# Windowed attention with its scores two blocks ahead, and the second key group projected one stage earlier

## The chip, the cores and the metric

The kernel runs on one core of a Trainium2 chip. The metric is the device time in microseconds from launch to end; the kernel before was run three times: 1077.41, 1073.83 and 1075.31, median 1075.31 us.

## The reference

One encoder layer over 1024 positions with 16 learned meta tokens ahead of them (T = 1040), model width 1024, everything in float32:

```python
u = _rms_norm(h, pre_w)
z = u @ w_in
rq, rk, rv, rg, aq, ak, av, ag, gr, ga = _split_in(z)
...
o_r = _bidirectional_retention(rq, rk, rv, lg_f, lg_b)      # 4 heads, forward and backward scan
...
y_r = (groupnorm(o_r) * ret_nw * silu(rg)) @ w_rb
...
aq = _rotary(aq) ; ak = _rotary(ak)                         # 8 query heads, 2 key groups, width 128
o_a = _windowed_sink_attention(aq, ak, av, sink)            # window +-128, meta keys, sink logit
y_a = (o_a * silu(ag)) @ w_ab
...
mix = sigmoid(gr) * y_r + sigmoid(ga) * y_a
return h + _rms_norm(mix @ w_o, post_w)
```

The attention takes, for each query, the keys within 128 positions and the 16 meta keys, adds a learned sink to the softmax's denominator and multiplies by the values of those keys.

## The kernel before

**Precision.** Each operand of TensorE is kept as a high part (type fp32r, made by a cast, on ScalarE as a rule) and a low part (made on VectorE by subtraction, `dve_lo`, line 90), and a product takes three matmuls: high by high, low by high, high by low (`mm3`, lines 74 to 76). What the text calls a step is one such group of three. A projection of 512 positions and 128 output columns is 8 steps (24 matmuls).

**Stages.** By the profile's times: set-up and first projection up to about 37 us; four retention heads up to 345 us; attention from 345 to 570 us; from there to 1066 us the gates and the three output products in a seven-product (Strassen-like) form; a short tail. The last retention head (head 3) runs from about 250 to 345 us.

**Attention.** There are 32 chunks: two key groups (g = 0, 1), and in each 16 blocks of 64 queries for the four heads of the group. A chunk has three stages.
- `stage1`: the scores. Two tiles `ps` on TensorE (six matmuls, in the two memory banks of the ring p2); VectorE adds the mask and takes the maximum (`raw`, `nm`, line 1366); ScalarE takes the exponential `p` (line 1369); VectorE inverts the sum (`den`, line 1372); GpSimd scales `p` (line 1379).
- `stage2`: the transposes `pt1`, `pt2` of p on TensorE (lines 1390, 1393; six instructions, in the two banks of the ring p1), then high parts on ScalarE (`pah`, `pbh`) and low parts on VectorE (`pal`, `pbl`). The banks come free for the next chunk when these four are done.
- `stage3`: p times values, `po` (nine matmuls, one bank), copied out by ScalarE (`oa`) and stored.

In TensorE's order the scores of chunk k+1 stand ahead of the transposes of chunk k. Then comes filler work, which does not depend on this chunk, and then `po` of chunk k-1. The filler is a list of generators (`works`), of which `fill(n)` issues n steps; `FILL` gives n for each chunk (7 or 8, in the last half 5). The list holds query projections (`paq`, from `gen_aq`), the projection of the second key group (`pak1`, from `gen_ak(1)`), and then products `pe` of the gates' weights (`gen_pre`, weights 6 to 13, each 24 matmuls), which the later stage loads back from DRAM.

Behind a step, the table `BEGUN` hangs other work: to fetch a weight (`fetch_aq`, `fetch_ak`), to split one half of it (`half_w`), to load, scale and subtract a piece of x and store it (`sum_fetch`, `sum_row`), to fetch a gate weight (`pre_fetch`: two transfers `we`), to sum its four parts (`pre_sums`, lines 785 to 787), and to split the sum (`pre_parts`: `weh` on ScalarE, line 794, then `wel` on VectorE). The two buffers for `we` are one pair: the next weight's transfers have to wait until this weight's sums and splits are done.

Queries are rotated (`rope_evac`: three multiplications on VectorE, lines 184 to 186, and an addition on GpSimd, line 187), stored to DRAM, and loaded again four heads at a time (`load_q`); `split_q` makes `aqh` on ScalarE (line 659) and `aql` on VectorE, two chunks before a pair of chunks needs them. Keys are rotated and split into `kT` (`keys`).

**What sets the order.** The kernel writes its own instruction order: each engine runs its queue in the order in which the program issues, and a pass that reorders within limits is bound by `issue_after` (`follow`), which puts an instruction's place behind that of others. SyncE (SP) issues nearly all transfers, in one queue.

Of the kernel before, what the change touches and what calls it, by code (L numbers as in the profile page):

```python
# [14 lines left out]
NM = 16  # L15
# [11 lines left out]
FILL = (7,) + (8,) * 6 + (7,) * 9 + (5,) * 15  # L27
# [12 lines left out]
def block_kernel(ctx: ExitStack, tc: tile.TileContext, xT, x, w_in, w_rb, w_ab, w_out, vecs, dec, sink,  # L40
# [68 lines left out]
    def halves_w(u):  # L109
        hi, lo = [], []  # L110

        def split(t, act):
            h, l = (wp.tile([P, 4, 256], R, tag=f"w{x}", bufs=4, name=f"w{x}{u}_{len(hi)}") for x in "hl")
            if act:
                nc.scalar.copy(h, t)
            else:
                pool_hi(h, t)
            dve_lo(l, t, h)
            hi.append(h)
            lo.append(l)  # L120

# [335 lines left out]
    def retention(h, fill):  # L457
# [137 lines left out]
        for c in range(NB, 0, -1):  # L595
# [67 lines left out]
    def fetch_aq(hp):  # L663
        raw = fetch_w(w_in, U_AQ + hp)
        split, wq[hp] = halves_w(U_AQ + hp)
        begun["q", hp] = lambda s: split(raw[s], True)

    def fetch_ak():
        raw = fetch_w(w_in, U_AK)
        split, w_ = halves_w(U_AK)  # L670
        wak.append(w_)
        begun["k", 1] = lambda s: split(raw[s], True)

    def half_w(which, i, s):
        begun[which, i](s)

    begun = {}

    def gen_aq(hp, i):
# [3 lines left out]
        for e_ in range(2):  # L683
            t = yield from proj(wq[hp], P * e_, a, b, f"paq{hp}_{i}{e_}")
            o = ra.tile([P, 512], F32, tag="q", bufs=6, name=f"aq{hp}_{i}{e_}")
            rope_evac(t, a, b, o, f"aq{hp}_{i}{e_}")
# [7 lines left out]
    rotated_k = {}  # L694

    def keys(g, i):
# [3 lines left out]
        kh, kl = (t[:, 2 * i:2 * i + 2, 0:P] for t in kT[g])  # L700
        o = rotated_k.pop((g, i))
        s = NM if i == 0 else 0
        x = o[:, s:s + 256].rearrange("p (t c) -> p t c", t=2)
        nc.scalar.copy(kh, x)
        dve_lo(kl, x, kh)
        if i == 0:
            mh, ml = (t[:, :, P:144] for t in kT[g])
            x = o[:, 0:NM].unsqueeze(1).to_broadcast([P, NB, NM])
# [18 lines left out]
    def sum_fetch(q):  # L727

        k, c = q // 2, slice(256 * (q % 2), 256 * (q % 2) + 256)
        for i in range(2):  # L730
            xsum[i] = t = ap.tile([P, 2, 256], F32, tag="xs", bufs=2, name=f"xs{i}{q}")
            nc.sync.dma_start(t, xT[4 * i + k, :, NM:T].rearrange("p (j t) -> p j t", j=2)[:, :, c])

    def sum_row(q):

        k, c = q // 2, slice(256 * (q % 2), 256 * (q % 2) + 256)
        x = {}
        for i, t in xsum.items():
            nc.scalar.activation(t, t, AF.Copy, scale=vec[:, 4 * i + k:4 * i + k + 1])
            for j in range(2):  # L740
                x[i, j] = t[:, j]
        for _, o, a, b in SUMS:
            nc.vector.tensor_tensor(x[o], x[a], x[b], ALU.subtract)
        for i, t in xsum.items():
# [44 lines left out]
    def pre_parts(u):  # L789
# [5 lines left out]
        dve_lo(l, t[:, :, 0:n], h)  # L795
        parts[u] = h, l

    def gen_pre(u):

        if u not in parts:  # L800
# [3 lines left out]
            pre_parts(u)  # L804
        h, l = parts.pop(u)
# [13 lines left out]
    def hooked(gens, at):  # L819

        n = 0
        for g in gens:
            for _ in g:
# [4 lines left out]
                yield  # L828
# [21 lines left out]
    for h in range(NH):  # L850
        fill, drain = filler([gen_qk(h + 1), pieces(pre, (4, 4, 8)[h])] if h < 3 else [gen_ak(0), gen_aq(0, 0), gen_aq(1, 0)])
# [476 lines left out]
    def attention():  # L1328
# [19 lines left out]
        def stage1(g, b):  # L1348
# [3 lines left out]
            den = ap.tile([P, 2], F32, tag="den", bufs=3, name=f"den{g}_{b}")  # L1352
            pt = []
            for e_ in range(2):
                hp, o0 = 2 * g + e_, 256 * (b % 2) + P * e_
                if (g, b // 2) not in aqs:
                    split_q(g, b // 2)
# [7 lines left out]
                p = ap.tile([P, 353], F32, tag="p", bufs=4, name=f"p{hp}_{b}")  # L1365
# [36 lines left out]
        def stage3(g, b):  # L1402
# [14 lines left out]
            if b % 2:  # L1417
# [6 lines left out]
        works = [gen_aq(1, 1), gen_aq(0, 1), gen_aq(2, 0), gen_aq(3, 0), gen_aq(2, 1), gen_aq(3, 1),  # L1424
                 gen_ak(1, (0, 1)), pieces(pre, 8), gen_ak(1, (2,)), pieces(pre, 8), gen_ak(1, (3,)), pre]
        fill = filler([hooked(works, BEGUN)])[0]
# [4 lines left out]
        with follow(last["pb"]):  # L1431
            next(av, None)
        edge_values(0, 0)
        edge_values(0, 1)

        with follow(*latest):
            fill(3)
        with follow(*latest):
            stage1(0, 0)
        for k, (g, b) in enumerate(chunks):  # L1440
            ends = k >= len(chunks) - 2
            if k + 1 < len(chunks):
                with follow(*latest, *marks("oa", "lo")):
                    stage1(*chunks[k + 1])
                if chunks[k + 1] == (0, 2 * NB - 1):
                    keys(1, 0)
            if k + 2 < len(chunks):
                edge_values(*chunks[k + 2])
            if chunks[k] == (1, 2 * NB - 2):

                with follow(*latest):
                    fill(FILL[k])
                yield
            if not k:
                with follow(*latest):
                    fill(FILL[k] - 3)
            with follow(*latest, *marks("exp", "sum")) if not ends else ExitStack():
                stage2(g, b)
            if k % 2 and k + 3 < len(chunks):
                g_, b_ = chunks[k + 3]  # L1460
                load_q(g_, b_ // 2)
            if k % 2 == 0 and k + 2 < len(chunks):
                g_, b_ = chunks[k + 2]
                with follow(*marks("exp", "sum", "lo", "hi")):
                    split_q(g_, b_ // 2)
            if k and not ends:
                with follow(*latest):
                    fill(FILL[k])
            with follow(*latest) if not ends else ExitStack():
                if k:  # L1470
                    stage3(*chunks[k - 1])
            if ends:
                yield
            if k in (12, 17, 21):
                x_to_out({12: 0, 17: 4, 21: 6}[k])
        stage3(*chunks[-1])


# [125 lines left out]
```

## Time and profile before

| | us |
|---|---|
| median of three runs | 1075.31 (1073.83 to 1077.41) |
| profiled execution | 1075.24 |
| its span, first to last instruction | 1073.5 |
| TensorE busy | 1049.6 (98%) |
| VectorE busy | 867.9 (81%) |
| ScalarE busy | 487.0 (45%) |
| GpSimd busy | 217.2 (20%) |
| mean granted TensorE clock | 0.995 |

The profiled execution is within 0.1 us of the median, and 1.74 us of it lie outside the span. The profile's engines are PE (TensorE), DVE (VectorE), ACT (ScalarE), POOL (GpSimd) and SP (the queue of transfers). In a table of windows each engine has its busy time and, in brackets, its instructions; then come the granted clock of PE, the share of the transfer engines that were busy, and GB/s. In a table of waits a row says which engine's instruction waited for whose result, the time in total, how often, and the longest.

### The profile page before, as it was taken

The page shows a single profiled execution, that of the slowest core. Times are in us where ns is not written, and L with a number is a line of the kernel's source. Part 1 is how long each engine was busy: PE and PEld are TensorE (multiplying, and loading weights), DVE is VectorE, ACT ScalarE, POOL GpSimd, SP SyncE. Part 2 cuts the span into 40 slices and gives each one's busy share as a digit, 9 for nine tenths or more (in the row PEclk, how much of TensorE's full clock was granted, in tenths as well). Part 3 has the DMA queues.
Part 4 walks back from the last instruction along what each step waited for, and adds up shares of the span by engine and source line. Part 5 has one row for each costly group of instructions (what it writes and reads, how often), then busy time and mean ns, then how long its engine had stood idle before and what let it go on. Part 6 is the DMA issues. An engine that isn't in the chain of part 4 may idle for free.

```text
span 1073.5 us, 17195 instructions
## 1 busy us (share of the span) xinstructions
PE 1049.6 (98%) x5863; PEld 905.7 (84%) x5863; DVE 867.9 (81%) x1770; ACT 487.0 (45%) x1064; POOL 217.2 (20%) x270
## 2 busy tenths in 40 slices
PE   8999999999999999989999999999999999999997
PEld 7898999989989788878888888888888888787886
DVE  7897788768986677787668988999799799767765
ACT  7141442422413444456557545555456546333432
POOL 3234225133352333342210000000000000110032
PEclk9999999999999999999999999999999999999999
DMA  7121111203131455576758769899934746789464
GB/s 285 40 70 43 57 41 60 84 28 102 51 108 49 140 178 178 166 241 223 220 169 272 265 232 313 275 360 345 377 129 157 241 172 221 234 206 326 122 118 78
DMA packets 109304, 187.14 MB, mean 174 GB/s; under 512 B 10864, under 2 KB 49648, under 8 KB 108400
## 3 DMA queue, kind: packets, MB, share of 16 engines
q1 hardware_dynamic: 105328, 179.47, 50.5%
q0 software_dynamic: 3456, 6.29, 3.9%
q8 instruction: 46, 0.75, 0.3%
q10 hardware_dynamic: 432, 0.28, 0.1%
q14 instruction: 42, 0.34, 0.1%
HBM read 124.92 MB, written 61.87 MB: 174 GB/s over the span
## 4 chain that ended last, share of the span: by engine, by line
PE 86%; DVE 6%; DMA 3%; issue 2%; ACT 2%; POOL 1%; SPq 0%; DVEq 0%; POOLq 0%; ACTq 0%
PE bz L75 8%; PE bz L74 8%; PE bz L76 8%; PE pv L74 3%; PE pv L75 3%; PE pv L76 3%; PE paq L75 3%; PE paq L76 3%; PE paq L74 3%; PE br L75 2%; PE br L74 2%; PE br L76 2%; PE bo L75 2%; PE bo L74 2%; PE bo L76 2%; PE ba L75 2%
## 5 line engine op out<-in xcount | busy, mean ns | idle before, releaser
L1210 POOL DMA_DIRECT2D mx_d<-c1a x4 | 3.7, 918 | 396.2 <-DVE c1a L1201 396.2
L75 PE MATMUL bz<-T,llz 128*128 128x512 f32 x192 | 75.7, 394 | 0.0
L76 PE MATMUL bz<-T,lhz 128*128 128x512 f32 x192 | 75.6, 395 | 0.0
L74 PE MATMUL bz<-T,lhz 128*128 128x512 f32 x192 | 75.4, 394 | 0.0
L74 PE MATMUL pv<-wh,big 128*128 128x256 f32 x256 | 73.2, 286 | 1.3 <-DVE m_qk L186 1.3
L75 PE MATMUL pv<-wh,big 128*128 128x256 f32 x256 | 73.2, 286 | 0.0
L76 PE MATMUL pv<-wl,big 128*128 128x256 f32 x256 | 72.5, 283 | 0.0
L75 PE MATMUL bz<-big,llz 128*128 128x512 f32 x176 | 69.7, 396 | 0.0
L76 PE MATMUL bz<-big,lhz 128*128 128x512 f32 x176 | 69.3, 394 | 0.0
L74 PE MATMUL bz<-big,lhz 128*128 128x512 f32 x176 | 68.6, 394 | 0.0
L1379 POOL TENSOR_SCALAR p<-p,den 128x352 f32<-128x352 f32 (+2 forms) x60 | 44.6, 757 | 92.7 <-DVE den L1372 88.4
L1369 ACT ACTIVATE p<-raw,nm 128x353 f32<-128x353 f32 (+2 forms) x64 | 36.0, 565 | 47.7 <-DVE nm L1366 46.8
L74 PE MATMUL paq<-big,wh 128*128 128x512 f32 x128 | 51.4, 402 | 0.0
L75 PE MATMUL paq<-big,wl 128*128 128x512 f32 x128 | 50.6, 396 | 0.0
L76 PE MATMUL paq<-big,wh 128*128 128x512 f32 x128 | 50.5, 394 | 0.0
L74 PEld LDWEIGHTS pv<-wh,big 128*128 128x128 f32 x256 | 48.3, 189 | 1.7 <-DVE m_qk L186 1.6
L75 PEld LDWEIGHTS pv<-wh,big 128*128 128x128 f32 x256 | 48.3, 189 | 0.2
L76 PEld LDWEIGHTS pv<-wl,big 128*128 128x128 f32 x256 | 48.3, 189 | 0.0
L1366 DVE CUSTOM_DVE_ANT_0 raw<-ps,mask,nsink 128x352 f32<-128x352 f32 (+2 forms) x64 | 33.4, 553 | 16.1 <-PE ps L76 15.8
L75 PEld LDWEIGHTS bz<-T,llz 128*128 128x128 f32 x192 | 36.2, 188 | 8.5
L74 PEld LDWEIGHTS bz<-T,lhz 128*128 128x128 f32 x192 | 36.2, 188 | 8.4
L76 PEld LDWEIGHTS bz<-T,lhz 128*128 128x128 f32 x192 | 36.2, 188 | 8.4
(620 smaller groups left out, 3574.4 us busy)
## 6 DMA issues: line engine op xcount, KB each, us to landing
wrz<-in_w_in_dram SPq DMA_DIRECT2D x32, 512.0 KB, 5.7
wr<-in_w_in_dram SPq DMA_DIRECT2D x31, 512.0 KB, 4.0
e<-e SPq DMA_DIRECT2D x40, 256.0 KB, 4.5
we<-in_w_in_dram SPq DMA_DIRECT2D x16, 512.0 KB, 5.2
tg<-tg_d SPq DMA_DIRECT2D x32, 256.0 KB, 5.1
T<-preT SPq DMA_DIRECT2D x6, 1024.0 KB, 7.1
oTr_d<-ost SPq DMA_DIRECT2D x16, 256.0 KB, 2.1
aq_d<-aq SPq DMA_DIRECT2D x16, 256.0 KB, 2.2
```

The lines of the kernel that those rows point to most:

```text
L74: nc.tensor.matmul(o, ah, bh, start=first, stop=False, **kw)
L75: nc.tensor.matmul(o, al, bh, start=False, stop=False, **kw)
L76: latest[:] = [nc.tensor.matmul(o, ah, bl, start=False, stop=last, **kw).ins]
L1210: nc.gpsimd.dma_start(d, to, accum_op=ALU.add)
L1366: nc.vector.tensor_tensor_reduce(raw[e_][:, 1:1 + wid], s[:, 0:wid], mask[:, mo:mo + wid], -SCALE, nsink[:, hp:hp + 1], ALU.add, ALU.min, ...
L1369: last["exp"] = nc.scalar.activation(p[:, 0:1 + wid], raw[e_][:, 0:1 + wid], AF.Exp, scale=-1.0, bias=nm_[:, e_:e_ + 1], accum_out=den[:, ...
L1379: nc.gpsimd.tensor_scalar(pt[e_][:, 0:wid], pt[e_][:, 0:wid], den[:, e_:e_ + 1], 1.0, op0=ALU.mult, op1=ALU.mult)
```

## The change

**Scores two ahead.** The scores of chunk k+2 are now issued behind the transposes of chunk k, between two pieces of filler; the scores of chunks 0 and 1 come before the loop. `FILL` holds two numbers for each chunk, counted in half steps (`(4, 4)` is two steps and two steps), so the attention has four steps in most chunks. To hold the additional chunk, `den` has four buffers for three, `p` six for four. `split_q` runs four chunks ahead, `load_q` six.

**Second key group in the last retention head.** All eight 512-wide projections of the queries of group 0 (heads `hp` 0 and 1) and the keys of both groups are projected as filler of head 3 (16 steps a chunk of its backward pass for 8): four `paq` and four `pak1` leave the attention. Key weights and query weights are each fetched once, so four transfers `wr` of 512 KB go, with four casts and four low parts. The rotated keys of group 1 go to DRAM (four stores), are loaded back in one transfer (`load_k`) and split behind the scores of chunks 15 and 16 in two pieces.

**Other work dealt anew.** `BEGUN` is a new table with less filler to hang on; `half_w` is called twice for each half, the cast first and the low part later; `sum_row` loses its scaling to `sum_scale`, `pre_parts` its low part to `pre_low`; the value projections `pav` up to the break in `gen_av` stand together ahead of the attention; x pieces (`xs`) move to another pool; three copies of x to the output are issued at other chunks. The banks of p2 are handed to the next stage earlier, and the products of that stage are interleaved differently with the last three chunks.

In TensorE's order around the transposes of group 0, block 14, there stands before (names are tiles with their buffer's number: the tile written, then the two read):

```order
L74 MATMUL ps1_15_6343<-kTh0_4314,aqh0_7_6183 128x208
L75 MATMUL ps1_15_6343<-kTh0_4314,aql0_7_6184 128x208
L76 MATMUL ps1_15_6343<-kTl0_4315,aqh0_7_6183 128x208
L1390 MATMUL pt1_0_14_6363<-ident_118,p0_14_6243 128x128
L1390 MATMUL pt1_0_14_6363<-ident_118,p1_14_6250 128x128
L1390 MATMUL pt1_0_14_6363<-ident_118,p0_14_6243 128x128
L1390 MATMUL pt1_0_14_6363<-ident_118,p1_14_6250 128x128
L1393 MATMUL pt2_0_14_6368<-ident_118,p0_14_6243 16x128
L1393 MATMUL pt2_0_14_6368<-ident_118,p1_14_6250 16x128
L74 MATMUL pak1_1_6383<-big0_0_109,wh12_0_6031 128x256
```

and in the changed kernel:

```order
L1409 MATMUL pt1_0_14_6491<-ident_118,p0_14_6350 128x128
L1412 MATMUL pt2_0_14_6496<-ident_118,p0_14_6350 16x128
L1409 MATMUL pt1_0_14_6491<-ident_118,p1_14_6357 128x128
L1409 MATMUL pt1_0_14_6491<-ident_118,p0_14_6350 128x128
L1409 MATMUL pt1_0_14_6491<-ident_118,p1_14_6357 128x128
L1412 MATMUL pt2_0_14_6496<-ident_118,p1_14_6357 16x128
L78 MATMUL ps2_0_6515<-kTh1_6448,aqh1_0_6332 128x208
L79 MATMUL ps2_0_6515<-kTh1_6448,aql1_0_6333 128x208
L78 MATMUL ps3_0_6524<-kTh1_6448,aqh1_0_6332 128x208
L79 MATMUL ps3_0_6524<-kTh1_6448,aql1_0_6333 128x208
L80 MATMUL ps2_0_6515<-kTl1_6449,aqh1_0_6332 128x208
L80 MATMUL ps3_0_6524<-kTl1_6449,aqh1_0_6332 128x208
```

Ahead of the transposes of block 14 stood the scores of block 15; now those of block 15 are a chunk back, and the scores of the next group's block 0 (`ps2_0`, `ps3_0`) follow the transposes; the filler behind them is no longer `pak1` but `pe`.

On VectorE, from the low part of gate weight 6 to the first sum of gate weight 7 (line 785), there stands before (the number behind a name is the tile's own; `we6` is gate weight 6):

```order
L90 TENSOR_TENSOR wel6_6285<-we6_1_6131,weh6_6284 128x1024
L90 TENSOR_TENSOR kTl1_6354<-akr1_0_6315,kTh1_6353 128x2x128
L90 TENSOR_TENSOR kTl1_6354<-akr1_0_6315,kTh1_6353 128x8x16
L743 TENSOR_TENSOR xs15_6195<-xs15_6195,xs05_6193 128x256
L1372 RECIPROCAL den0_15_6335<-den0_15_6335 128x2
L90 TENSOR_TENSOR pal0_14_6372<-pt1_0_14_6363,pah0_14_6371 128x512
L90 TENSOR_TENSOR pbl0_14_6374<-pt2_0_14_6368,pbh0_14_6373 16x256
L1364 COPY raw2_6430<-nsink_102 128x1
L1364 COPY raw3_6439<-nsink_102 128x1
L90 TENSOR_TENSOR aql1_0_6380<-qf1_0_6276,aqh1_0_6379 128x512
L743 TENSOR_TENSOR xs15_6195<-xs15_6195 128x256
L785 TENSOR_TENSOR we7_1_6292<-we7_0_6291,we7_1_6292 128x4x128
```

and in the changed kernel, where that sum is line 799:

```order
L94 TENSOR_TENSOR wel6_6298<-we6_1_6108,weh6_6297 128x1024
L190 TENSOR_TENSOR m1_aq3_11_6374<-paq3_11_6253,cr_119 128x512
L191 TENSOR_TENSOR m2_aq3_11_6375<-paq3_11_6253,sr_120 64x512
L192 TENSOR_TENSOR m2_aq3_11_6375<-paq3_11_6253,sr_120 64x512
L1391 RECIPROCAL den0_14_6345<-den0_14_6345 128x2
L94 TENSOR_TENSOR pal0_13_6402<-pt1_0_13_6393,pah0_13_6401 128x512
L94 TENSOR_TENSOR pbl0_13_6404<-pt2_0_13_6398,pbh0_13_6403 80x256
L757 TENSOR_TENSOR xs06_6257<-xs06_6257 128x256
L1385 ISA raw0_5011,nm0_15_6429<-ps0_15_6431,mask_3800,nsink_102 128x208
L1385 ISA nm0_15_6429 128x1
L799 TENSOR_TENSOR we7_1_6262<-we7_0_6261,we7_1_6262 128x4x128
L1385 ISA raw1_5012,nm0_15_6429<-ps1_15_6438,mask_3800,nsink_102 128x208
```

Between the two there are now the last query rotation and the scores' maximum of block 15; the second `raw` of that block stands behind the sum, and so behind what the sum waits for.

On TensorE at the end of the attention, behind the last scores (group 1, block 15) stood:

```order
L74 MATMUL ps3_15_7642<-kTh1_6353,aqh1_7_7521 128x208
L75 MATMUL ps3_15_7642<-kTh1_6353,aql1_7_7522 128x208
L76 MATMUL ps3_15_7642<-kTl1_6354,aqh1_7_7521 128x208
L74 MATMUL pe13_3_7652<-big1_0_110,weh13_7534 128x512
L75 MATMUL pe13_3_7652<-big1_0_110,wel13_7535 128x512
L76 MATMUL pe13_3_7652<-big1_1_112,weh13_7534 128x512
```

where twelve matmuls of `pe13_3` came ahead of the transposes of block 14; and now:

```order
L78 MATMUL ps3_15_7605<-kTh1_6448,aqh1_7_7409 128x208
L79 MATMUL ps3_15_7605<-kTh1_6448,aql1_7_7410 128x208
L80 MATMUL ps3_15_7605<-kTl1_6449,aqh1_7_7409 128x208
L1412 MATMUL pt2_1_13_7669<-ident_118,p3_13_7500 80x128
L78 MATMUL po1_12_7680<-pah1_12_7539,vah_558 128x256
L79 MATMUL po1_12_7680<-pah1_12_7539,val2_5009 128x256
```

The products `pe13_3` are now done before the last scores, and nine matmuls `po` of block 12 stand between these and the transposes of block 14.

The diff, cut to its core:

```diff
-FILL = (7,) + (8,) * 6 + (7,) * 9 + (5,) * 15
+START = 6, 6
+FILL = (((5, 6),) * 1 + ((5, 5),) * 1 + ((4, 4),) * 1 + ((4, 3),) * 1 + ((4, 5),) * 2 + ((4, 7),) * 1 + ((4,
...
+            if act == "apart":
+                return lambda: dve_lo(l, t, h)
+            dve_lo(l, t, h)
...
-                    fill(KT)
+                    fill(KT if h < NH - 1 else 2 * KT)
...
     def half_w(which, i, s):
-        begun[which, i](s)
+        if (which, i, s) in low_w:
+            low_w.pop((which, i, s))()
+        else:
+            low_w[which, i, s] = begun[which, i](s)
...
+    def load_k():
+        later_k.append(aw.tile([P, T], F32, tag="kf", bufs=1, name="kf"))
+        nc.sync.dma_start(later_k[0], ak_d)
...
-            o = rotated_k[g, i] = ra.tile([P, 272], F32, tag="ak", bufs=2, name=f"akr{g}_{i}")
+            o = ra.tile([P, 272], F32, tag="ak", bufs=2, name=f"akr{g}_{i}")
             rope_evac(t, a, b, o, f"ak{g}_{i}")
-            if not g:
-                keys(g, i)
+            if g:
+                nc.sync.dma_start(ak_d[:, a:b], o[:, 0:b - a])
+            else:
+                s = NM if i == 0 else 0
+                keys(g, i, o[:, s:s + 256], None if i else o[:, 0:NM])
...
+    def pre_low(u):
+        h, l, t = parts[u]
+        dve_lo(l, t, h)
         parts[u] = h, l
...
-    ... else [gen_ak(0), gen_aq(0, 0), gen_aq(1, 0)])
+    ... else [gen_ak(0), gen_ak(1), gen_aq(0, 0), gen_aq(0, 1), gen_aq(1, 0), gen_aq(1, 1)])
...
-            den = ap.tile([P, 2], F32, tag="den", bufs=3, name=f"den{g}_{b}")
+            den = ap.tile([P, 2], F32, tag="den", bufs=4, name=f"den{g}_{b}")
...
-                p = ap.tile([P, 353], F32, tag="p", bufs=4, name=f"p{hp}_{b}")
+                p = ap.tile([P, 353], F32, tag="p", bufs=6, name=f"p{hp}_{b}")
...
-        works = [gen_aq(1, 1), gen_aq(0, 1), gen_aq(2, 0), gen_aq(3, 0), gen_aq(2, 1), gen_aq(3, 1),
-                 gen_ak(1, (0, 1)), pieces(pre, 8), gen_ak(1, (2,)), pieces(pre, 8), gen_ak(1, (3,)), pre]
+        works = hooked([(gen_aq(2, 0), 2), (gen_aq(3, 0), 2), (gen_aq(2, 1), 2), (gen_aq(3, 1), 2), (pre, 2)], BEGUN)
...
+        for k in range(len(chunks)):
+            ends = len(chunks) - 3 - k
+            if not ends:
+                scores(k + 2)
                 with follow(*latest):
+                    fill(1000)
                 yield
+            with follow(*latest, *marks("exp", "sum")) if ends > 0 else ExitStack():
+                stage2(*chunks[k])
+            query_step(k)
+            if ends > 0:
                 with follow(*latest):
+                    fill(FILL[k][0])
+                scores(k + 2)
                 with follow(*latest):
+                    fill(FILL[k][1])
+            if k:
+                with follow(*latest) if ends > 0 else ExitStack():
                     stage3(*chunks[k - 1])
...
+             56: [(sum_fetch, 6), (pre_fetch, 7)], 57: [(pre_sums, 6)], 58: [(pre_parts, 6)],
+             59: [(pre_low, 6)], 62: [(sum_scale, 6)], 64: [(sum_row, 6)], 65: [(pre_sums, 7), (pre_fetch, 8)],
...
+    free.extend(["p2", "p2"])
```

More of the change, by code (lines that the diff above doesn't have):

```diff
@@ L804, in gen_pre @@
             pre_parts(u)
+        if len(parts[u]) > 2:
+            pre_low(u)
         h, l = parts.pop(u)
@@ L821, in hooked @@
         n = 0
-        for g in gens:
+        for g, cost in gens:
             for _ in g:
@@ L1457, in attention @@
[L1457 to L1466, printed above, removed]
+                    fill(FILL[k][0])
@@ L1513, in block_kernel @@
     next(steps)
+    next(i)
+    next(steps)
     for _ in i:
```

149 lines of the change are left out of this document (80 added, 69 removed).

## The prediction

> **What bounds the kernel now.** I read the page's busy times first, then its chain, then the attention cut into windows, then the waits inside it. The page:
>
> ```profile
> PE 1049.6 (98%) x5863; PEld 905.7 (84%) x5863; DVE 867.9 (81%) x1770; ACT 487.0 (45%) x1064; POOL 217.2 (20%) x270
> ...
> PE 86%; DVE 6%; DMA 3%; issue 2%; ACT 2%; POOL 1%; SPq 0%; DVEq 0%; POOLq 0%; ACTq 0%
> ```
>
> TensorE carries the chain, and the changed kernel issues the same 5863 matmuls. So a gain can only come from time in which PE stands still or runs at a lower clock; the span of 1073.5 us holds 23.9 us of idle PE. The attention (columns: window, length, busy PE, PEld, DVE, ACT, POOL, clock, share of the transfer engines, GB/s) has more than a third of it:
>
> ```profile
> 345.00:365.00 20.00, 18.41 (x115) 15.98 (x114) 9.36 (x28) 9.90 (x27) 2.32 (x5) 1.00 0.38 106
> 365.00:455.00 90.00, 89.94 (x494) 77.87 (x493) 70.64 (x143) 41.37 (x100) 34.60 (x35) 1.00 0.57 174
> 455.00:510.00 55.00, 49.53 (x315) 44.59 (x315) 43.24 (x110) 31.79 (x82) 17.86 (x20) 0.94 0.73 231
> 510.00:570.00 60.00, 58.34 (x337) 50.53 (x336) 37.89 (x91) 35.92 (x91) 11.91 (x17) 1.00 0.66 201
> sum 225.00, PE 216.22 PEld 188.97 DVE 161.13 ACT 118.98 POOL 66.69; mean PE 54.06 PEld 47.24 DVE 40.28 ACT 29.74 POOL 16.67
> ```
>
> 225.00 - 216.22 = 8.78 us idle, 5.47 of them in the 55 us from 455 to 510, where the clock is 0.94 besides. Cut finer, that stretch shows two spells at half clock, each behind a gap in PE's work:
>
> ```profile
> 460.70:463.30 2.60, 0.29 (x4) 0.14 (x3) 2.12 (x6) 2.60 (x9) 0.99 (x2) 1.00 0.40 122
> ...
> 464.90:468.15 3.25, 3.25 (x18) 3.25 (x16) 3.25 (x10) 2.77 (x9) 0.55 (x3) 0.50 0.49 152
> ...
> 481.20:482.80 1.60, 0.23 (x3) 0.02 (x2) 1.09 (x5) 1.60 (x6) 0.72 (x2) 1.00 0.65 216
> ...
> 485.40:488.70 3.30, 3.30 (x18) 3.21 (x16) 1.08 (x4) 2.87 (x7) 1.10 (x2) 0.50 0.76 242
> ```
>
> They cost (3.25 + 3.30) x 0.50 = 3.28 us, if PE had done that work at full clock. So 8.78 + 3.28 = 12.06 us is what the attention can give. PE's waits there, all of them:
>
> ```profile
> PE ps L74 <- ACT aqh L659: 3.0, 3, 1.4
> PE pt L1390 <- DVE pal L90: 2.3, 1, 2.3
> PE ps L75 <- DVE aql L90: 1.2, 3, 0.6
> PE pt L1390 <- POOL p L1379: 0.9, 2, 0.7
> PE pt L1390 <- POOL akr L187: 0.5, 1, 0.5
> PE ps L74 <- DVE nm L1366: 0.3, 1, 0.3
> PE pt L1393 <- DVE pbl L90: 0.3, 1, 0.3
> ```
>
> **The change, part by part.**
>
> *Queries split four chunks ahead* take away 3.0 + 1.2 = 4.2 us: scores waited for `aqh` and `aql`, which were made two chunks ahead on engines that run behind. Two chunks more are over 10 us, and the longest of these waits is 1.4 us.
>
> *Scores two chunks ahead* take away the 0.9 us of `pt` on `p`: a chunk and its filler now lie between, where 0.7 us were short. With `pak1` gone from the attention, the 0.5 us on `akr` goes as well. Two small waits I leave in the sum, since the change keeps their places: `ps` on `nm` at the start, where the second scores wait for the two banks of p2, and one `pbl`. That is 0.3 + 0.3 = 0.6 us to put back (bounds: nothing, and 1.2 if both double).
>
> *The wait of 2.3 us on `pal`* is DVE running late. From 455 us on it stood in front of sums that wait for transfers:
>
> ```profile
> DVE we L785 <- DMA we<-in_w_in_dram: 9.0, 5, 2.8
> ...
> DMA to landing us min/median/max: 3.6/5.2/6.5
> ```
>
> Nine us in five waits, and behind each one, in order, stand the low parts that free PE's banks. What of it goes depends on the two parts that follow.
>
> *Work moved to head 3.* Four `paq` (96 matmuls) and four `pak1` (96, half as wide) leave the attention. They join a stage in which PE does not wait at all and DVE is nearly full:
>
> ```profile
> 300.00:320.00 20.00, 20.00 (x98) 16.69 (x97) 16.84 (x30) 1.83 (x4) 10.31 (x10) 1.00 0.40 132
> 320.00:340.00 20.00, 20.00 (x163) 19.32 (x162) 16.15 (x47) 5.81 (x16) 7.48 (x13) 1.00 0.15 53
> ```
>
> There PE's own work hides the retention's chain; doubling the filler adds cover. The wide matmul's pace is in these rows, from the first of twelve to the instruction behind the last:
>
> ```profile
> 566.00 0.41 PE L74 MATMUL pe<-big,weh 128*128 128x512 f32 x1
> ...
> 568.80 0.60 PE L1390 MATMUL pt<-ident,p 128*128 128x128 f32 x4
> ```
>
> 2.80 / 12 = 0.233 us, so 96 are 22.4 us, and the keys, half as wide, some 12: about 35 us of PE, with this on DVE (groups of the attention; busy us, mean ns of one):
>
> ```profile
> L186 DVE TENSOR_TENSOR m_aq<-paq,sr 64x512 f32<-64x512 f32 x12 | 8.3, 694 | 0.2
> ...
> L186 DVE TENSOR_TENSOR m_ak<-pak,sr 64x256 f32<-64x256 f32 x3 | 1.3, 427 | 0.0
> ```
>
> Four times three at 0.69 and four times three at 0.43 are 8.3 + 5.2 = 13.5 us of DVE for 35 of PE, 39%, where the stage now has 82%: DVE gets looser there, not tighter. GpSimd's additions, eight, find it at most half busy. Cost: 0. If that cover fails, the bound is the 13.5 us of DVE; nothing in these rows points to it. The four stores, one load and four weight fetches fewer are off every wait that PE shows, so 0 also; the same holds for the low parts that go with the fetches, which lay in 365 to 455, where PE lost 0.06 us. The reload of the keys is needed only at the scores of chunk 16, dozens of us after the stores.
>
> *Attention gets shorter, so everything else in it comes closer.* In the stage of `pe` a chunk had five steps, now four. From the chain of before:
>
> ```profile
> 548.08 0.44 PE pt L1390 x4
> 554.26 0.44 PE pt L1390 x4
> 560.31 0.44 PE pt L1390 x4
> ```
>
> (560.31 - 548.08) / 2 = 6.12 us for a chunk, less three matmuls, 0.70, makes 5.42. A gate weight feeds 24 matmuls, two chunks: PE wants a new one each 10.83 us. Each one is made by a loop: its two transfers, three sums on DVE, the cast, the low part, and only then are its buffers free for the next. The last links, by the groups (mean ns), and two periods of the loop, from end to end of `wel`, by the timeline of DVE:
>
> ```profile
> L785 DVE TENSOR_TENSOR we<-we,we 128x512 f32<-128x512 f32 x8 | 5.5, 687 | 9.0 <-DMA we<-in_w_in_dram 9.0
> L90 DVE TENSOR_TENSOR wel<-we,weh 128x1024 fp32r<-128x1024 f32 x8 | 9.8, 1222 | 0.6
> L794 ACT CAST weh<-we 128x1024 fp32r<-128x1024 f32 x8 | 8.4, 1046 | 1.0 <-DVE we L787 1.0
> ...
> 465.34 1.22 DVE L90 TENSOR_TENSOR wel<-we,weh 128x1024 fp32r<-128x1024 f32 x1
> 475.72 1.23 DVE L90 TENSOR_TENSOR wel<-we,weh 128x1024 fp32r<-128x1024 f32 x1
> 492.36 1.21 DVE L90 TENSOR_TENSOR wel<-we,weh 128x1024 fp32r<-128x1024 f32 x1
> 504.33 1.23 DVE L90 TENSOR_TENSOR wel<-we,weh 128x1024 fp32r<-128x1024 f32 x1
> ```
>
> At the least the loop takes 5.2 + 3 x 0.69 + 1.05 + 1.22 = 9.5 us plus the issue; it was seen at 475.72 - 465.34 = 10.38 and at 504.33 - 492.36 = 11.97. (The others were longer, where the old table asked for a weight only every 10 to 14 steps; the new one asks for seven in 56 steps, eight apart as PE uses them.) I take the mean of the two, 11.18: seven periods, each 0.35 us longer than PE's 10.83, make 2.4 us. Bounds: 0 at 10.38, and 8.0 at 11.97.
>
> *The tail.* `pe13_3`, 2.80 us by the rows at 566, covered the last softmax and the first work of the next stage on DVE; now nothing does. DVE is nearly full behind it, while PE does not wait:
>
> ```profile
> 570.00:595.00 25.00, 25.00 (x117) 20.08 (x116) 24.11 (x41) 19.44 (x39) 0.00 (x0) 1.00 0.91 300
> 595.00:620.00 25.00, 25.00 (x109) 20.23 (x109) 24.21 (x41) 12.77 (x23) 0.00 (x0) 1.00 0.75 245
> ```
>
> Its free time there is 0.89 + 0.79 = 1.68 us. What the lost cover exceeds, 2.80 - 1.68 = 1.1 us, I take as PE's new wait; bounds 0 and 2.8.
>
> *The clock.* In both cases above a gap (2.31 us, and 1.37) came 1.6 and 2.6 us ahead of a half-clock spell. The sum has one wait of that kind left, at the first `pe` products of weight 7, where the first `we` sum on DVE stands between the two `raw` of block 15. Half a spell, 0.8 us; bounds 0 and 3.28, the two of before. [...]
>
> Sum: 1075.24 (the profiled execution, 0.07 under the median) - 12.06 + 0.6 + 2.4 + 1.1 + 0.8 = 1068.1 us.
>
> **Rivals.**
>
> A. *All waits go.* 1075.24 - 12.06 = 1063.2. For it: PE lost 0.06 us in the 90 us from 365 to 455, with the old order. Against it: the loop of weights at 10.38 is its best period.
>
> B. *The weights' loop becomes the bound.* Without its term the sum is 1065.7, and seven periods of c us each give 1065.7 + 7 x (c - 10.83). At 11.97 that is 1073.7, inside the noise; from c = 12.66 on the kernel is slower than before by over 0.3%, and at 13 it is 1080.9. For it: DVE works in order, a wait for the transfer holds up all that stands behind it, the chunk's `raw` and `pal` too; the transfers of the next weight start only when this `wel` is done; 6.5 us for a landing is in the row. Against it: DVE has 13.5 us and four low parts less to do.
>
> C. *The transposes' banks.* From `pt` to the next `pt` there were 6.12 us, now 5.42; ahead of `pal` stand the cast and what DVE still has queued. If each of the 13 chunks of that stage waited 0.5 us more, 6.5 us, the time is 1074.6, no change. For it: the 2.3 us of before. Against it: it was one wait in 32 chunks.
>
> D. *The half-clock spells are not due to the gaps* and stay: 1068.1 - 0.8 + 3.28 = 1070.6. For it: two cases are few, and no row shows what the granted clock answers to. Against it: both spells follow within 3 us of the two longest gaps. [...]
>
> That the change leaves the waits in place isn't likely: 4.2 of the 8.5 us are on the split of queries, which now stands two chunks earlier.
>
> **How the numbers follow.** 0.3% is 3.2 us, about what a measurement of this kernel can tell from no change: under 1072.1 is faster, over 1078.5 slower. Chances: the sum as forecast 0.52 (its own range 1064.5 to 1072, from the weights' loop at 10.6 to 11.7), A 0.08, D 0.06, B between 11.75 and 12.66 us 0.10, C 0.07, B beyond that 0.17. Faster is then 0.66, no change 0.17, slower 0.17. The range runs from A, a little below, to the edge of the slower case: 1062.5 to 1078.0.
>
> **What would show it.** In the profile after: no row of `ps` on `aqh` or `aql` and none of `pt` on `p`; a stretch of the attention some 35 us shorter and head 3 that much longer, PE idle in neither; `wel` to `wel` between 10.4 and 11.7 us, and waits of `pe` on `wel` of 1 to 4 us in all; at most 2 us of wait between the last scores and the next stage; clock 0.995 or above. It is wrong if `pe` waits for `wel` in each weight, if DVE's waits for `we` exceed the 9.0 us of before, if `pal` holds up the transposes in many chunks, or if PE waits in head 3.

## The result, and the profile after

The changed kernel took 1067.59 us (median of five runs, 1066.20 to 1069.26), the kernel before 1074.97 us beside it: a ratio of 0.9932, 95% interval 0.9914 to 0.9951. Measured again in experiment 9, the ratio was 0.9941 (0.9930 to 0.9953). The forecast was 1068.1 us, 0.9934 of the execution that it was worked out from. The profiled execution took 1069.26 us, its span is 1067.5 us; it was the longest of the five.

The page after, busy time and chain:

```profile
PE 1046.2 (98%) x5863; PEld 904.3 (85%) x5863; DVE 860.0 (81%) x1764; ACT 481.7 (45%) x1058; POOL 206.5 (19%) x270
...
PE 89%; DVE 5%; DMA 3%; issue 1%; ACT 1%; POOL 0%; SPq 0%; DVEq 0%; POOLq 0%; ACTq 0%
```

The span is 6.0 us shorter (1073.5 to 1067.5): 2.6 us of it is idle time (23.9 to 21.3), 3.4 us is PE's busy time (1049.6 to 1046.2). Only half of the latter is a better clock. The two spells at half clock are gone from the attention; they last 3.41 us each by the trace's record of the clock, and so cost 3.4 us. But this execution has one of 3.41 us in the set-up, from 37.11 us, which costs 1.7 us. The other 1.7 us are not traced; the scores' instructions alone (`ps`) were busy for 34.86 us in place of 36.38. The first scores now start at 388.35 us (352.77 before), so these windows, with the same columns as before, hold the end of head 3 too:

```profile
345.00:380.00 35.00, 35.00 (x236) 31.79 (x235) 17.60 (x35) 8.59 (x19) 7.34 (x6) 1.00 0.45 145
380.00:455.00 75.00, 75.00 (x452) 67.17 (x451) 55.35 (x137) 41.30 (x105) 22.40 (x30) 1.00 0.54 162
455.00:480.00 25.00, 22.90 (x139) 19.62 (x138) 23.28 (x56) 15.93 (x43) 7.63 (x10) 1.00 0.66 208
480.00:510.00 30.00, 26.30 (x142) 22.01 (x143) 18.45 (x47) 15.87 (x40) 7.49 (x10) 1.00 0.85 263
510.00:540.00 30.00, 30.00 (x185) 27.16 (x184) 23.39 (x56) 21.31 (x54) 5.96 (x11) 1.00 0.69 205
540.00:570.00 30.00, 29.42 (x183) 26.02 (x182) 20.11 (x50) 18.98 (x51) 3.90 (x8) 1.00 0.67 213
sum 225.00, PE 218.62 PEld 193.77 DVE 158.18 ACT 121.99 POOL 54.72; mean PE 36.44 PEld 32.30 DVE 26.36 ACT 20.33 POOL 9.12
```

None of these windows has a clock below 1.00, where before the stretch from 455 to 510 had 0.94. 225.00 - 218.62 = 6.38 us are still idle, all but 0.6 us of them between 455 and 510 us, where DVE is busy for 23.28 of 25 us first. PE's waits there:

```profile
PE pe L79 <- DVE wel L94: 3.0, 3, 1.4
PE pt L1409 <- POOL p L1398: 1.7, 2, 1.4
PE po L78 <- ACT oa L1434: 0.5, 1, 0.5
PE ps L78 <- DVE nm L1385: 0.5, 1, 0.5
PE ps L80 <- DVE kTl L94: 0.4, 1, 0.4
PE pe L78 <- ACT weh L808: 0.2, 1, 0.2
```

All waits on `aqh`, `aql`, `pal`, `pbl` and `akr` are gone. New are those on `wel` (the low part of a gate weight), as forecast; the wait on `p`, forecast to go, is now longer. On DVE, four of the eight `wel` and two waits between them (timeline; start, length, in brackets the idle time ahead):

```profile
465.51 1.22 DVE L94 TENSOR_TENSOR wel<-we,weh 128x1024 fp32r<-128x1024 f32 x1
479.25 1.21 DVE L94 TENSOR_TENSOR wel<-we,weh 128x1024 fp32r<-128x1024 f32 x1
487.19 0.89 DVE L757 TENSOR_TENSOR xs<-xs,xs 128x256 f32<-128x256 f32 x2 [3.86 <-ACT xs L750]
492.46 1.22 DVE L94 TENSOR_TENSOR wel<-we,weh 128x1024 fp32r<-128x1024 f32 x1
499.62 0.69 DVE L799 TENSOR_TENSOR we<-we,we 128x512 f32<-128x512 f32 x1 [2.83 <-DMA v<-val]
502.87 1.23 DVE L94 TENSOR_TENSOR wel<-we,weh 128x1024 fp32r<-128x1024 f32 x1 [1.12 <-ACT weh L808]
```

The first two periods are 13.74 and 13.21 us, the third 10.41, and the others, to 546.06, between 10.3 and 11.2: PE wants one each 10.83 us, so the lateness is made in the first two; the third wait on `wel`, 0.8 us at 503 us, is what is left of it.

### The profile page after: what moved, and what is told of

Read it like the earlier page. It is cut to its first block, busy times and chain, and to the rows that moved or that the text cites. A ratio compares the mean times of both kernels' runs of the same rounds, so it can differ in the third digit from the quotient of the medians.

```text
span 1067.5 us, 17154 instructions
## 1 busy us (share of the span) xinstructions
PE 1046.2 (98%) x5863; PEld 904.3 (85%) x5863; DVE 860.0 (81%) x1764; ACT 481.7 (45%) x1058; POOL 206.5 (19%) x270
## 4 chain that ended last, share of the span: by engine, by line
PE 89%; DVE 5%; DMA 3%; issue 1%; ACT 1%; POOL 0%; SPq 0%; DVEq 0%; POOLq 0%; ACTq 0%
PE bz L79 8%; PE bz L78 8%; PE bz L80 8%; PE pv L78 3%; PE pv L79 3%; PE pv L80 3%; PE ba L79 2%; PE br L79 2%; PE paq L79 2%; PE paq L78 2%; PE paq L80 2%; PE br L80 2%; PE br L78 2%; PE ba L78 2%; PE ba L80 2%; PE bo L78 2%
## 5 line engine op out<-in xcount | busy, mean ns | idle before, releaser
L1398 POOL TENSOR_SCALAR p<-p,den 128x352 f32<-128x352 f32 (+2 forms) x60 | 36.8, 626 | 111.2 <-DVE den L1391 102.3
L595 ACT ACTIVATE ost<-to,rnw 128x128 f32<-128x128 f32 x64 | 19.9, 364 | 69.7 <-PE to L590 54.5
```

The source lines that it names most:

```text
L595: nc.scalar.activation(ost[0][:, e_, w0:w0 + P], to[:, P * e_:P * e_ + P], AF.Copy, scale=rnw[:, 2 * h + e_:2 * h + e_ + 1])
L1398: nc.gpsimd.tensor_scalar(pt[e_][:, 0:wid], pt[e_][:, 0:wid], den[:, e_:e_ + 1], 1.0, op0=ALU.mult, op1=ALU.mult)
```

## The experiments

The ratios below are to the kernel before on the same chip; the changed kernel is at 0.993 to 0.994 by them.

**1. The split of queries one chunk later.**

```diff
-            if k % 2 == 0:
-                if k + 4 < len(chunks):
-                    g, b = chunks[k + 4]
+            if k % 2:
+                if k + 3 < len(chunks):
+                    g, b = chunks[k + 3]
```

> The changed kernel, with the queries split and loaded one chunk later, about as far ahead of their scores as before. Theory (the split's lead was worth the 4.2 us of waits on aqh and aql in the profile before): waits of the scores on aqh or aql come back, 2 to 4.2 us in all, and the time is 1070 to 1073 us; if a gap of over 1 us comes back, a half-clock spell follows it. Rival (with some 18 us of VectorE work gone from the attention the split would be in time anyhow): no such waits, 1066 to 1069 us.

Ratio 0.9961 (0.9945 to 0.9976), 1073.16 us. No wait on `aqh` or `aql` came back, so the theory's reason is wrong although its time came out. The waits are of the changed kernel's kinds at other sizes, with none on `p`, but the profiled execution has two stretches at a lower clock:

```profile
455.00:480.00 25.00, 23.34 (x140) 20.80 (x138) 22.50 (x56) 14.57 (x39) 7.53 (x10) 0.93 0.68 205
480.00:510.00 30.00, 27.52 (x136) 22.80 (x135) 19.44 (x47) 18.00 (x45) 6.26 (x10) 0.90 0.84 265
```

25 x 0.07 + 30 x 0.10 = 4.8 us. Of its ten runs the three with a mean clock of 0.997 or more took 1069.6 to 1070.4 us, the others 1071.6 to 1076.0. Why the spells came oftener here isn't settled; the last section has waits of this size with a spell behind them and without.

**2. Scores one chunk ahead again,** all else as changed.

```diff
+            if ends >= 0:
+                scores(k + 1)
...
                     fill(FILL[k][0])
-                scores(k + 2)
```

> The changed kernel, with each chunk's scores issued one chunk ahead of their transposes again, as before (the last two chunks excepted); the split of queries, the work moved to the last retention head and the new table stay. Theory (two chunks ahead was worth only the waits of the transposes on p, 0.9 us before): 1067.5 to 1070 us, pt waits on p for 1 to 3 us. Rival (with five per cent less work in each chunk, one chunk ahead would no longer cover the softmax): pt waits on p in most chunks, 0.3 us and more each, 1075 us and above.

Ratio 1.0061 (1.0038 to 1.0083), 1081.67 us: slower than the kernel before, and 13 us slower than the changed one. By its time the rival is right, not by its reason; the waits on `p` are few, and most of the time is waited for two results of DVE (the four longest rows):

```profile
PE pe L79 <- DVE wel L94: 4.3, 3, 2.6
PE pt L1409 <- DVE pal L94: 3.2, 3, 2.2
PE pt L1409 <- POOL p L1398: 2.0, 2, 1.8
PE pe L78 <- ACT weh L808: 1.4, 1, 1.4
```

Its span is 11.6 us longer: 8.2 of it idle, 3.4 PE's busy time. Two spells of 3.41 us at half clock cost it 3.4 us, the one of the changed kernel's profile 1.7, so the clock is half of that difference.

**3. The low part of gate weights 7 to 13 made twice.**

```diff
         h, l, t = parts[u]
+        if u > 6:
+            dve_lo(l, t, h)
         dve_lo(l, t, h)
```

> The changed kernel, with the low part of gate weights 7 to 13 computed twice on VectorE, the second time over the first, so the loop of transfer, sums, cast and low part is 1.2 us longer for seven weights; the result is the same. Theory (this loop binds the second half of the attention, as rival B priced it): seven periods 1.2 us longer, less what is free in the later ones, 5 to 8.5 us more than the changed kernel, 1073 to 1076 us, with waits of pe on wel of 7 us and more. Rival (only the first two weights were late, through other work in VectorE's queue; the others have slack): 1 to 3 us more, 1068.5 to 1071 us.

Ratio 1.0081 (1.0057 to 1.0105), 1085.24 us, some 16 us more than the changed kernel for 8.5 us of work on DVE. `pe` waited for `wel` at each of the seven weights:

```profile
PE pe L79 <- DVE wel L94: 13.3, 7, 3.3
```

That is 10.3 us more than in the changed kernel, and two windows of 30 us at a clock of 0.89 add 30 x 0.11 x 2 = 6.6 us. So the theory's mechanism holds, a longer loop is paid for at every weight, but the time is 9 us above its range: the price, like rival B's, left out the clock.

**4. The sums of the last piece of x later.**

```diff
-             66: [(sum_fetch, 7), (pre_parts, 7)], 67: [(pre_low, 7)], 72: [(sum_scale, 7)],
-             73: [(sum_row, 7), (pre_sums, 8), (pre_fetch, 9)], 74: [(pre_parts, 8)], 76: [(pre_low, 8)],
+             66: [(sum_fetch, 7), (pre_parts, 7)], 67: [(pre_low, 7)], 73: [(pre_sums, 8), (pre_fetch, 9)],
+             74: [(pre_parts, 8)], 76: [(pre_low, 8)], 77: [(sum_scale, 7)], 79: [(sum_row, 7)],
```

> The changed kernel, with the scaling and the sums of the last piece of x five and six steps later. In the profile after, ScalarE waited 4.7 us for that piece's load and VectorE 3.9 us for the scaling, ahead of the sums of gate weight 8. Theory (that wait made the transposes wait 1.4 us for p at 492 us and pe 0.8 us for wel at 493.7): both go, 2 to 3 us less, 1064.5 to 1065.8 us. Rival (the transfer of gate weight 8, issued only when the low part of weight 7 was done, would have held VectorE as long): VectorE waits for we in place of xs, at most 1 us less, 1066.5 to 1068 us.

Ratio 0.9935 (0.9917 to 0.9954): nothing gained. DVE's wait of 3.9 us for `xs` went, and its waits ahead of the weights' sums rose from 6.3 us (3.5 for the weights' transfers, and the 2.8 shown above) to this, while `pe` waited 4.8 us for `wel`:

```profile
DVE we L799 <- DMA we<-in_w_in_dram: 10.8, 5, 4.9
```

The rival is right: behind the wait removed stood the next one.

**5. The kernel before, with the split of queries one chunk earlier,** and for that one more step of filler in the first chunk and the first two splits ahead of the loop.

```diff
-FILL = (7,) + (8,) * 6 + (7,) * 9 + (5,) * 15
+FILL = (8,) * 7 + (7,) * 9 + (5,) * 15
...
+            split_q(0, 0)
             next(av, None)
+        split_q(0, 1)
...
-            if k % 2 and k + 3 < len(chunks):
-                g_, b_ = chunks[k + 3]
+            if k % 2 == 0 and k + 4 < len(chunks):
+                g_, b_ = chunks[k + 4]
                 load_q(g_, b_ // 2)
-            if k % 2 == 0 and k + 2 < len(chunks):
-                g_, b_ = chunks[k + 2]
+            if k % 2 and k + 3 < len(chunks):
+                g_, b_ = chunks[k + 3]
...
                     split_q(g_, b_ // 2)
```

> The kernel before, with one thing changed: queries are loaded and split one chunk earlier (one more step of filler in the first chunk makes them ready in time). Theory (the prediction's 4.2 us of waits of ps on aqh and aql go with the lead alone): those waits are gone and the kernel is 3 to 5 us faster than before. Rival (ScalarE and VectorE are late there whatever they split; the first run of this study, where the lead was taken back, showed no wait on aqh): the waits move to nm, p or pal, and the time is within 1.5 us of before.

Ratio 0.9999 (0.9991 to 1.0008). The waits on `aqh` and `aql` are gone, 4.2 us of them, and nothing is won, because these came in their place (the kernel before had 2.3, 0.9, none, 0.3 and 0.3 us in the same rows):

```profile
PE pt L1390 <- DVE pal L90: 3.3, 4, 1.6
PE pt L1390 <- POOL p L1379: 2.4, 2, 2.1
PE ps L76 <- DVE kTl L90: 1.1, 1, 1.1
PE pt L1393 <- DVE pbl L90: 0.9, 2, 0.7
PE ps L74 <- DVE nm L1366: 0.4, 1, 0.4
```

**6. The kernel before, with scores two chunks ahead,** the split as far ahead of the scores as it was. In this kernel the keys of group 1 are split right ahead of their first scores, since their projection isn't done earlier.

```diff
+                    fill(n // 2)
+                if k + 2 < len(chunks) - 1:
+                    scores(k + 2)
...
+                    fill(n - n // 2)
```

> The kernel before, with scores two chunks ahead as in the changed kernel, and the queries split as far ahead of their scores as before; no work moves to the last retention head, and the filler steps stay, halved around the scores. Theory (two chunks ahead is what the gain comes from, as its removal in the changed kernel cost 13 us): 4 us and more faster than before. Rival (it is worth only the 0.9 us of transposes on p as long as a chunk has its old filler; it is the shorter chunk of the changed kernel that needs it): within 2 us of before.

Ratio 0.9974 (0.9964 to 0.9985), 2.8 us faster, between theory and rival. What is left of its waits is mostly the keys:

```profile
PE ps L74 <- ACT kTh L709: 3.3, 1, 3.3
PE ps L74 <- DVE nm L1366: 1.5, 1, 1.5
PE ps L76 <- DVE kTl L90: 1.1, 1, 1.1
PE pt L1390 <- POOL p L1379: 1.0, 2, 0.8
```

Scores two chunks ahead need the keys a chunk earlier; with the second group projected in the attention these are not there. So the two halves of the change need each other: the rest without the scores' lead is 0.6% slower than before, the lead without the rest 0.3% faster, with 4.4 us of waits on the keys still in it, and both together 0.6 to 0.7% faster. The rest itself was not taken apart: no run separates the work moved to head 3 from the new table.

**7. A gate weight's two transfers in the other order.**

```diff
-        for j, t in enumerate(reversed(raw)):
-            nc.sync.dma_start(t[:, :, 0:n], w_in[gates[u], :, 4 - 4 * j:8 - 4 * j, 0:n])
+        for t, k in zip(raw, (0, 4) if len(raw) > 1 else (4,)):
+            nc.sync.dma_start(t[:, :, 0:n], w_in[gates[u], :, k:k + 4, 0:n])
```

> The changed kernel, with the two transfers of each gate weight in the other order: first the one whose buffer is free after the sums of the weight before, then the one that waits for its low part. Theory (the loop's transfer is late because both are issued only after the low part): the first lands earlier, VectorE's waits for we fall below the 3.5 us of the profile after, wel to wel of the first periods falls from 13.7 and 13.2 us by about 1 us each, 1 to 2.5 us less, 1065 to 1066.5 us. Rival (the second transfer sets the sums all the same): 1067 to 1069 us.

Ratio 0.9946 (0.9932 to 0.9959): no gain. `wel` to `wel` is 13.38 and 13.58 us in the first periods, the same two waits on `wel` and on `p` stand at 480 and 492 us.

**8. `pe13_3` behind the last scores again.** The last chunks of `FILL` get fewer half steps.

```diff
-        ((4, 4),) * 4 + ((5, 4),) * 1 + ((3, 4),) * 1 + ((4, 4),) * 1)
+        ((4, 4),) * 2 + ((4, 2),) * 1 + ((4, 2),) * 1 + ((4, 3),) * 1 + ((3, 3),) * 1 + ((4, 2),) * 1)
```

> The changed kernel, with the last three chunks' filler cut by four steps, so that twelve matmuls of pe13_3 stand behind the last scores again, as before. Theory (the prediction's tail term: the lost cover costs 1.1 us; the profile after shows 0.5 us of po on oa there): the wait on oa goes, 0.3 to 1.1 us less, 1066.5 to 1067.3 us. Rival (the cover is then missing in the three chunks ahead, whose transposes wait): 1068 to 1071 us.

Ratio 0.9914 (0.9901 to 0.9927), 1066.90 us: the wait of `po` on `oa` is gone and no other kind has come in the attention, as the theory has it. But a wait of 1.0 us (`bz` on `u2z`) stands at 658 us that the first profile of the changed kernel doesn't have, and PE is idle for 22.5 us in all against 21.3 there; that execution is shorter by 0.65 us all the same, at a mean granted clock of 0.998 for 0.997. So the gain is not traced to the tail. It is the fastest kernel of the study, 0.2 to 0.3% under the changed kernel, with intervals that overlap the first measurement of that and just miss the second; experiment 10 has the same tail and shows no gain.

**9. The changed kernel again,** beside the two that follow.

> The changed kernel as it is, beside the kernel before on the chip of the next runs. Expected by its first measurement: 0.993 of before, 1067 to 1069 us, waits of pe on wel at weights 7 and 8 and of the transposes on p at 492 us as in the profile after, no half-clock spell in the attention or a short one.

Ratio 0.9941 (0.9930 to 0.9953), 1069.36 us. The waits were where they had been, but for `nm` (1.1 us for 0.5) and the third on `wel` (gone); 1.49 us on `p` at 491 and 0.77 on `wel` at 492.8, for 1.43 and 0.77 in the first profile. This time a half-clock spell followed (0.68 and 0.50 in the windows 492 to 494 and 494 to 496), which the first profile doesn't have.

**10. Three edits together:** the order of experiment 7, the tail of experiment 8, and the sums of the last two pieces of x far later (scaling and sums at steps 84, 86, 100 and 102 for 62, 64, 72 and 73).

```diff
-             59: [(pre_low, 6)], 62: [(sum_scale, 6)], 64: [(sum_row, 6)], 65: [(pre_sums, 7), (pre_fetch, 8)],
-             66: [(sum_fetch, 7), (pre_parts, 7)], 67: [(pre_low, 7)], 72: [(sum_scale, 7)],
-             73: [(sum_row, 7), (pre_sums, 8), (pre_fetch, 9)], 74: [(pre_parts, 8)], 76: [(pre_low, 8)],
+             59: [(pre_low, 6)], 65: [(pre_sums, 7), (pre_fetch, 8)],
+             66: [(pre_parts, 7)], 67: [(pre_low, 7)],
+             73: [(pre_sums, 8), (pre_fetch, 9)], 74: [(pre_parts, 8)], 76: [(pre_low, 8)], 84: [(sum_scale, 6)],
+             86: [(sum_row, 6)], 87: [(sum_fetch, 7)], 100: [(sum_scale, 7)], 102: [(sum_row, 7)],
```

> The changed kernel, with three edits together: pe13_3 behind the last scores (faster alone), the two transfers of a gate weight in the other order (no gain alone), and the sums of the last two pieces of x 22 to 34 steps later, out of the stretch from 465 to 500 us (moving the last one alone gave nothing, since the wait for the weight's transfer took its place). Theory (there the first two weights are late for two reasons side by side, VectorE's work and the transfers; with both lightened the weights are in time): wel to wel 11 to 12 us in the first two periods for 13.7 and 13.2, pe waits on wel for 0 to 1 us in place of 3.0, pt on p under 0.5, 3 to 4 us less than the changed kernel, 1063 to 1065 us. Rival (the stretch is bound by VectorE's necessary work, keys and masks included): 1065 to 1068 us.

Ratio 0.9950 (0.9938 to 0.9962), 1070.18 us: the theory falls, and the time lies above the rival's range too, which is the nearer one. The first two periods of `wel` did fall, to 12.60 and 10.20 us; but the work put off has to be done, and the waits went along with it:

```profile
PE pe L79 <- DVE wel L94: 3.2, 3, 1.2
PE pt L1409 <- DVE pal L94: 1.2, 2, 1.0
PE pe L78 <- ACT weh L808: 0.8, 1, 0.8
PE ps L78 <- DVE nm L1385: 0.3, 1, 0.3
```

The periods from 499 to 538 us became 12.8, 12.7 and 12.8 us, and PE's idle time there, which had been nothing from 510 to 540, became 2.4 us.

**11 and 12. Gaps made on purpose,** at two places where PE had not waited; the second kernel has 11 and 14 for 10 and 12.

```diff
-            dve_lo(al[:, 0:w], t1[:, 0:w], ah[:, 0:w])
+            for _ in range({(0, 4): 10, (0, 10): 12}.get((g, b), 1)):
+                dve_lo(al[:, 0:w], t1[:, 0:w], ah[:, 0:w])
```

> The changed kernel, with the low part pal computed 10 times in chunk 4 and 12 times in chunk 10 of the first group (same result each time), which makes VectorE 6.2 and 7.6 us late at two places where PE did not wait; PE's gaps there should be 0 to 2 and 1 to 3 us. Theory, from the gaps seen so far (all six of 2.2 us and more were followed by half clock, most of the shorter ones were not): half clock for about 3.3 us behind a gap of 2.2 us or more, none behind one under 1.2 us. [...]

> As the run before, with pal computed 11 and 14 times: VectorE 6.9 and 9.0 us late, PE's gaps 0.5 to 2.5 and 2.5 to 5 us. Theory: a half-clock spell behind the second gap, and behind the first if it is 2.2 us or more. [...]

The gaps were longer than meant: 3.03 and 4.01 us in the first, 3.03, 4.00 and 4.30 us in the second, and the times, one run each, 1081.34 and 1086.03 us. All five were followed by a half-clock spell. The first of the second kernel, in windows:

```profile
419.00:422.00 3.00, 0.02 (x1) 0.00 (x0) 2.98 (x8) 1.46 (x4) 1.24 (x2) 0.82 0.29 76
422.00:425.00 3.00, 2.94 (x8) 2.41 (x9) 2.97 (x7) 0.37 (x1) 0.00 (x0) 0.50 1.67 487
425.00:427.00 2.00, 2.00 (x8) 1.94 (x7) 1.11 (x3) 0.13 (x1) 0.00 (x0) 0.50 0.03 7
427.00:429.00 2.00, 2.00 (x10) 1.62 (x9) 1.36 (x4) 1.23 (x4) 0.00 (x0) 0.81 0.74 259
429.00:432.00 3.00, 3.00 (x22) 2.74 (x21) 2.44 (x6) 1.74 (x4) 1.60 (x2) 1.00 0.40 109
```

The clock fell inside the gap (0.82 over its 3 us) and stayed at half for 6.83 us, from 420.93 to 427.76, in a stage that has 1.00 throughout in the changed kernel. This gap of 3.03 us so cost 3 us and half of the 5.7 us of work that PE did in this spell.

## Why the prediction was right, and where it was not

**The bound and the sum.** Right in the main: the idle time and the half clock came out of the attention. Against the forecast of 12.06 us to be had and 4.9 us to be given back (0.6, 2.4, 1.1, 0.8), 6.4 us of idle time and no clock loss were left in the profiled execution: 1075.24 - 12.06 + 6.4 = 1069.6, measured 1069.26. Two things that the sum doesn't have nearly cancel in this: the spell in the set-up, 1.7 us, and 1.7 us less of busy time at full clock, although the same matmuls were to take the same time. The step "a gain can only come from time in which PE stands still or runs at a lower clock" is short by the latter.

**Work moved to head 3 at no cost.** Right: its windows are full (45.00 of 45 us from 300 to 345, and 110.00 of 110 from there to 455), and PE's waits between 250 and 380 us are two of 0.6 and 0.5 us that the profile before has too. DVE was busy for 39.41 of 50 us from 300 to 350, 79%, a little looser than the 82% from 300 to 340 before.

**"Queries split four chunks ahead take away 4.2 us"** failed as a step of its own. Alone it gave nothing (experiment 5), and taken back it brought no such wait (experiment 1). The row named what came last, not what was short: with `aqh` and `aql` early, PE met other late results, of DVE for the most part, in the same stretch. The changed kernel has neither these nor those; which part of its new order or lighter load did that, no run shows. (The lead also grew by less than the step says: the scores themselves moved a chunk forward, so the split gained about a chunk and a half on them, not two.)

**"Scores two chunks ahead take away the 0.9 us"** failed twice: the wait on `p` grew to 1.7 us, and the part was worth far more than its row, 13 us within the changed kernel (experiment 2). Without it PE waited for `wel`, `pal`, `p`, `weh`, `pah` and `lhz`, so it seems to cover the lateness of several engines and not one wait, and a kernel with four steps of filler in a chunk needs that.

**The weights' loop, 2.4 us.** The mechanism was right, the size was 3.2 us, and its shape was different: not seven periods each a little too long but the first two at 13.7 and 13.2 us, the others in time. Experiment 3 shows that it has next to no slack; experiments 4, 7 and 10 suggest that its first periods are made by DVE's work and by the transfers side by side, since lightening one of them changed little. Rival B's condition (12.66 us in all periods) was not met.

**The tail, 1.1 us,** was 0.5 us (`po` on `oa`); experiment 8 removed that wait. **The start and the banks, 0.6 us:** the waits at these places are gone, and two others came at the second group's first scores (0.5 on `nm`, 0.4 on `kTl`), which the sum didn't have.

**The clock, 0.8 us,** was 0 in the attention of the first profile and 1.7 us (3.41 us at 0.50) in that of experiment 9. Rival D (spells that don't come from gaps) is refuted for the attention by experiments 11 and 12, where half clock followed all five gaps of 3.03 to 4.30 us, in places that have 1.00 without them.

So the median was right to 0.5 us, and the profiled execution to 1.2 us, with two of the steps wrong. What PE would still wait for and lose at half clock in the attention was about right as a whole, 4.9 us forecast and 6.4 measured. That the terms add up so closely is in part luck: the waits on `p` (1.7 us, forecast to go) and at the second group's first scores (0.9) stand against a smaller tail and a clock term of nothing.

## What to carry to other kernels

A row of waits names the result that came last; when the engine behind it is late for more than that, taking that wait away brings the next one, so price such waits together, by the load of the late engine in that stretch, and test one of them alone before counting on it. Parts of a schedule change can need each other: here the lead of the scores was worth 0.3% alone (there with keys that came late) and some 1.2% beside the shorter chunks, and the shorter chunks without it were a loss. In the traces of this case a long gap of PE cost more than its length: half clock followed each of the twelve single gaps of 2.23 us and more in the attention (next section), so the work behind such a gap belongs into its price.

## What was not expected of the hardware

Over all traces of this case, each single gap of PE of 2.2 us or more in the attention was followed by a half-clock spell: twelve of twelve, from 2.23 us (experiment 2) to 4.30 us (experiment 12). Two single gaps of 2.11 us (experiment 5) and 2.12 us (experiment 3) were not. Behind shorter gaps a spell came or not: the pair of 1.43 to 1.51 us and 0.77 us, which the changed kernel has at 489 to 494 us, was followed by a spell in experiments 7 and 9, and by none in the first profile and in experiment 8.

The trace's record of the clock shows more. Each spell in the attention lasts 3.41 or 6.83 us. Those of experiment 3 begin at 483.06, 496.71 and 510.37 us, 13.65 us apart, those of experiment 11 at 421.61, 462.57 and 503.53 us, 40.96 us apart: four times and twelve times 3.413 us. Here are three stretches around the pair of gaps in the first profile, then two in experiment 9, the second of which is its spell:

```profile
487.66:491.08 3.42, 2.87 (x17) 2.37 (x16) 3.42 (x9) 2.44 (x9) 2.17 (x2) 1.00 0.52 180
491.08:494.49 3.41, 1.76 (x9) 1.31 (x10) 2.68 (x7) 3.29 (x8) 1.40 (x3) 1.00 0.92 275
494.49:497.90 3.41, 3.41 (x18) 2.91 (x18) 2.11 (x6) 1.89 (x7) 0.53 (x1) 1.00 0.94 252
489.32:492.73 3.41, 1.20 (x8) 0.65 (x6) 3.41 (x9) 2.59 (x6) 1.64 (x1) 1.00 0.86 246
492.73:496.14 3.41, 3.36 (x9) 2.88 (x10) 1.08 (x3) 1.17 (x4) 1.10 (x2) 0.50 0.89 197
```

In the first profile PE is idle for 0.55 us in the first of the three and for 1.65 us in the second, and the clock stays at 1.00; in experiment 9 it is idle for 2.21 us in the first of the two, and the second has 0.50. So 2.2 us of idle time in the same two waits had a spell behind them in one execution and none in the other; what decides it was not shown. The time of a run of one kernel goes in part with its clock: of the kernel before, the two of twenty runs on one chip with a mean clock of 0.998 took 1072.6 and 1073.0 us, those at 0.993 from 1075.6 to 1081.0.
